# A two-layer trunk with eight experts on one core: earlier sums, transposed turns and four pieces ahead of the routing

## The chip, the cores and the metric

The kernel runs on one NeuronCore of a Trainium2 chip. The metric is the device time of one execution in microseconds (us), from the program's start to its end; lower is better. TensorE (PE in the profile; PEld is its weight load), VectorE (DVE), ScalarE (ACT), GpSimd (POOL) and SyncE (SP) run their own instruction lists and wait for each other by semaphores. SP issues the transfers of the weights.

## What is computed

Two layers over 256 latent and 256 context tokens of width 1024. Layer 0 ends in a dense feed-forward part, layer 1 in eight experts of which each latent token takes two. The change lies in the experts of layer 1 and in what stands right ahead of them:

```python
def swiglu(h, wg, wu, wd):
    return (jax.nn.silu(h @ wg) * (h @ wu)) @ wd

def moe_ffn(h, w_r, wg, wu, wd):
    logits = (h @ w_r).astype(jnp.float32)
    top_v, top_i = lax.top_k(logits, TOP_K)               # TOP_K = 2
    gates = jax.nn.softmax(top_v, axis=-1)
    combine = jnp.sum(jax.nn.one_hot(top_i, N_EXPERTS, dtype=jnp.float32) * gates[..., None], axis=-2).astype(h.dtype)
    out = jnp.zeros_like(h)
    for e in range(N_EXPERTS):                            # N_EXPERTS = 8
        out = out + combine[..., e:e + 1] * swiglu(h, wg[e], wu[e], wd[e])
    return out
...
x = x + mod[5] * f        # f = moe_ffn(hf, ...), hf of 256 x 1024; wg, wu 1024 x 2816, wd 2816 x 1024
```

## The kernel before

The first 878 us or so hold both layers up to the last output projection; then the routing ranks the experts by the number of their tokens, and from about 900 us on the experts run.

**Places.** The program is fixed while the routing is not, so experts are put on eight places with a capacity of slots each: place 0 has 160 slots (128, and 32 more that are called the rest, number NE), places 1 and 2 have 128, 3 to 5 have 64, 6 and 7 have 32. Place 7 is always expert 0, so its weights can be loaded before the routing is known. `gather` makes a place's tokens (`xe`) by one-hot products; AHEAD names the chunk at which each gather of a group of places begins.

**Chunks and pieces.** The 2816 hidden columns of an expert are 11 chunks of 256. A chunk takes three pieces of 1 MiB: two of gate and up (`gu`), one of down (`dn`); 264 pieces in all. SP issues them in the order of use (`Weights._load`, L240) into a ring of raw buffers: 4, and 5 more from one pool, hold pieces ahead of the routing, 3 more come with a pool that opens after it (`more`). For a wide place (128 slots) each piece is split in halves into a high part by ACT (`whi`, L275) and a low part by DVE (`wlo`, L276), in two pairs of buffers (tags `hi` and `lo`); a half is split when it is due. Narrow (32) and middle (64) places use the raw pieces.

**Rounds.** RUNS sets the order: `(None, (4, 0))` is four rounds with narrow chunks alone; `(1, (6, 11))` is run 1, the 11 chunks of place 1 with 6 narrow chunks (places 7, then 6) and 11 middle ones (3, 4, 5) spread over them; then run 0 and run 2, and two narrow rounds at the end. A round does the wide chunk's gate-up, the down product of the wide chunk of the round before, then narrow and middle gate-ups and the down products of the former round's, then the turns.

**Turns.** The gate-up of a narrow or middle chunk leaves its values folded over the partitions. They are copied to SBUF (`mid`), turned by TensorE into a bank `mTx` (`turn`: a product with the constant `sel` for 32 slots, which adds two folds on the way, and a transpose for 64), and made into `silx` by ACT's silu and DVE's product (`turned`, L1589). The wide chunk's `sil` is transposed into a bank `mT` and split into `mh` (ACT) and `ml` (DVE, L438).

**Finishes.** A place's down products add up over 11 chunks in a bank: `py` (two, one wide place at a time), `pys` (one, a middle place) or `pyx` (one, a narrow place). After the last, `finishes` is put among the side tasks, one finish at a time over all places (`finishing`). It multiplies the sum by mod5 (`y`, L1766 for wide, L1770 for others), splits it (`yh`, `yl`), and for each half and each 128 tokens scatters it by a one-hot product (`sc`, two banks by turns) that DVE adds to `acc` by the gate (L1780). A side task is moved on whenever the main order polls; where its instructions come in an engine's list is then fixed by the planner's clock (`o.clk`).

Of the kernel before, what the change touches and what calls it, by code (L numbers as in the profile page):

```python
# [18 lines left out]
P = 128  # L19
# [195 lines left out]
class Weights:  # L215


    def __init__(self, net, items, nraw, nhi):
# [3 lines left out]
        self.raw_live = self.hi_live = self.half = 0  # L222
        self.ring, self.at_ring = [(net.wp, nraw)] * nraw, 0
# [6 lines left out]
    def _load(self):  # L230
# [6 lines left out]
        pool, bufs = self.ring[self.at_ring]  # L237
        self.at_ring = (self.at_ring + 1) % len(self.ring)
        t = pool.tile([P, WW if pool is net.wp else 2048], F32, tag="raw", name="wraw", bufs=bufs)
# [7 lines left out]
    def more(self, pool, n):  # L247

        a = self.at_ring
        self.ring = self.ring[:a] + [(pool, n)] * n + self.ring[a:]  # L250
        self.nraw += n

# [88 lines left out]
class Net:  # L341
# [1150 lines left out]
    def onehot(self, p):  # L1492

        nc = self.nc
        yield from until(lambda: len(self.ohT) < 2)
# [10 lines left out]
        ohT = self.mp.tile([P, 2, P], F32R, tag="ohT", name="ohT", bufs=2)  # L1506
# [5 lines left out]
    YB, YH = 1, 1  # L1512
# [63 lines left out]
    def turn(self, pt, at, v, m):  # L1576
        for j in range(2):
            b = v[:, P * j:P * j + P]
            if m == 32:
                self.mm(pt[:, at + 64 * j:at + 64 * j + 64], b, self.sel, True, True)  # L1580
            else:
                self.tp(pt[:, at + P * j:at + P * j + P], b)

    def turned(self, pt, at, m):

        src = pt[:, at:at + 4 * m].rearrange("p (j g s) -> p j g s", j=2, g=2)
# [5 lines left out]
    def experts(self):  # L1592
# [6 lines left out]
        self.finishing = False  # L1599
        self.ndone = 0  # L1600
        self.sel = self.mp.tile([P, 64], F32, name="sel", bufs=1)
        nc.vector.tensor_tensor(self.sel, self.c("ident", 0, 64), self.c("swap", 0, 64), op=ALU.add)
        o.spawn(self.gather(0), 2)
        pw, pn = None, []
        for w, ns in self.rounds() + [(None, [])]:
# [71 lines left out]
            if mids:  # L1677
                pt, at = self.bank("mTx"), 0
                for *_, m, v in mids:
                    self.turn(pt, at, v, m)  # L1680
                    at += 4 * m
            pw = None
            if w:
                pm = self.bank("mT")
                for j in range(2):
                    self.tp(pm[:, P * j:P * j + P], sil[:, P * j:P * j + P])
                mh = self.mp.tile([P, 256], F32R, tag="mh", name="mh", bufs=1)
                ml = self.mp.tile([P, 256], F32R, tag="ml", name="ml", bufs=1)
                self.split(mh, ml, pm[:, :256])
                pw = [*w, mh, ml, None]  # L1690
            at = 0
            for p, c, m, v in mids:
                mx = self.turned(pt, at, m)
                at += 4 * m
                if p == NE:
                    pw[4] = mx
                else:
                    pn.append((p, c, mx))
            yield

    def down(self, p, c, mh, ml):
# [12 lines left out]
        if z and p:  # L1714
            self.o.spawn(self.finishes(p), 1)
        return w

    def down_rest(self, w, c, mx):
# [13 lines left out]
        if c == NCH - 1:  # L1732
            self.o.spawn(self.finishes(0), 1)

    def down_small(self, p, c, mx):
# [8 lines left out]
        if c == NCH - 1:  # L1744
            self.o.spawn(self.finishes(p), 1)

    def finishes(self, p):
        yield from until(lambda: not self.finishing)
        self.finishing = True
        for q in (p, NE) if p == 0 else (p,):  # L1750
            yield from self.finish(q)
        self.finishing = False

    def finish(self, p):

        nc = self.nc
        m = self.slots(p)
        parts = P // m
        w = 512 if m > 32 else 256
        yield from until(lambda: self.ohT.get(p) is not None)  # L1760
        ohT = self.ohT[p]
        for n in range(2 if m == P else 1):
            yh, yl = (self.mp.tile([P, 512], F32R, tag=nm, name=nm, bufs=self.YH) for nm in ("yh", "yl"))
# [8 lines left out]
            yield 3.0  # L1772
# [172 lines left out]
```

## Time and profile before

| | us |
|---|---|
| median of 3 runs | 1585.33 (1581.52 to 1587.26) |
| profiled execution | 1583.83 |
| its span, first to last instruction | 1582.1 |
| mean granted TensorE clock, as a share of full speed | 0.978 |
| TensorE, VectorE, ScalarE busy | 1500.2, 821.2, 666.7 |
| one MoE piece, issue to landing, median | 12.6 |

The rows are of one profiled execution. A busy row gives an instruction group's start and its length in us, engine, line, operation, output and inputs; the bracket at the end is the idle time before it on that engine and what ended it. TensorE's ends are modelled, so its pitch from start to start is safer than its lengths. [...]

### The profile page before, as it was taken

Reading aid. Unit: us, or ns where it says so; the run is one execution under the profiler, and the core shown is the slowest. Engines: PE = TensorE matmul, PEld = TensorE weight load, DVE = VectorE, ACT = ScalarE, POOL = GpSimd, SP = SyncE. Lnnn points to the kernel's source line nnn. Section 1 sums busy time; section 2 is a strip of 40 time slices with the busy share of each in tenths; the row PEclk is TensorE's granted clock in tenths of the full one; section 3 lists DMA queues with packets and bytes.
Section 4 is the critical chain, followed back from the end, with each engine's and each line's share of the span. In section 5 each row is a group of like instructions: output and inputs, shape, how many; then the busy total and the mean of one; then the engine's idle time right before and its main releaser. Section 6 shows DMA issues by size and latency. Waiting matters only on the chain. (4 is left out here: it accounts for less than half of the span.)

```text
span 1582.1 us, 23498 instructions
## 1 busy us (share of the span) xinstructions
PE 1500.2 (95%) x9302; PEld 1081.1 (68%) x9303; DVE 821.2 (52%) x1481; ACT 666.7 (42%) x1189; POOL 102.6 (6%) x135
## 2 busy tenths in 40 slices
PE   5999998899999999999999899999999999999997
PEld 1766675787887787878757776666566666656654
DVE  2687568543232333378774344544465444654545
ACT  3566644443222312266455354444343443433441
POOL 1200123210000000030300000000000000000000
PEclk9999999999999999999999899999999999999998
DMA  9422055333323323333164499999998999999994
GB/s 372 152 106 107 28 211 202 133 133 112 129 91 149 133 107 113 112 141 142 56 267 181 152 418 419 419 419 420 418 390 358 371 413 417 419 402 407 419 420 158
DMA packets 57715, 396.10 MB, mean 250 GB/s; under 512 B 6528, under 2 KB 8576, under 8 KB 10496
## 3 DMA queue, kind: packets, MB, share of 16 engines
q1 hardware_dynamic: 56016, 392.03, 62.2%
q10 hardware_dynamic: 1584, 2.52, 0.4%
q8 instruction: 75, 1.23, 0.3%
q14 instruction: 40, 0.33, 0.1%
HBM read 393.47 MB, written 1.05 MB: 249 GB/s over the span
## 5 line engine op out<-in xcount | busy, mean ns | idle before, releaser
L276 DVE TENSOR_TENSOR wlo<-wraw,whi 128x1024 fp32r<-128x1024 f32 (+2 forms) x318 | 377.0, 1222 | 161.2 <-ACT whi L275 155.9
L275 ACT ACTIVATE whi<-wraw 128x1024 fp32r<-128x1024 f32 (+2 forms) x318 | 320.0, 1047 | 148.5 <-PE fd L374 57.9
L374 PE MATMUL gu<-whi,xw 128*128 128x512 f32 x528 | 169.1, 401 | 4.2 <-ACT whi L275 4.2
L374 PE MATMUL gu<-wraw,xs 128*64 128x256 f32 (+1 forms) x1760 | 166.2, 386 | 0.5 <-ACT xs L1484 0.5
L374 PEld LDWEIGHTS gu<-wraw,xs 128*64 128x64 f32 (+1 forms) x1760 | 94.4, 127 | 64.3 <-issue 14.6
L374 PEld LDWEIGHTS gu<-whi,xw 128*128 128x128 f32 x528 | 96.9, 190 | 24.5 <-ACT whi L275 6.1
L374 PE MATMUL gu<-wlo,xw 128*128 128x512 f32 x264 | 104.9, 397 | 3.5 <-DVE wlo L276 3.5
L1162 DVE TENSOR_TENSOR fsil<-fsil,fu 128x512 f32<-128x512 f32 x22 | 15.1, 688 | 153.5 <-PE fu L374 118.2
L374 PE MATMUL pys<-wraw,silx 128*32 128x256 f32 (+1 forms) x616 | 87.6, 480 | 6.8 <-DVE y L1770 4.1
L425 ACT ACTIVATE fsil<-fg 128x512 f32<-128x512 f32 x22 | 13.1, 598 | 174.3 <-PE fg L374 174.3
L1573 ACT ACTIVATE mid<-gu 128x256 f32<-128x256 f32 x55 | 21.0, 382 | 137.1 <-PE gu L374 137.1
L374 PE MATMUL fg<-ahi,whi 128*128 128x512 f32 (+1 forms) x192 | 72.3, 377 | 0.0
L374 PE MATMUL fg<-alo,whi 128*128 128x512 f32 (+1 forms) x192 | 71.6, 373 | 0.2 <-POOL alo L523 0.2
L374 PE MATMUL fg<-ahi,wlo 128*128 128x512 f32 (+1 forms) x192 | 71.4, 372 | 0.0
L374 PE MATMUL fu<-alo,whi 128*128 128x512 f32 (+1 forms) x192 | 71.4, 372 | 0.0
L374 PE MATMUL fu<-ahi,wlo 128*128 128x512 f32 (+1 forms) x192 | 71.3, 372 | 0.0
L374 PE MATMUL fu<-ahi,whi 128*128 128x512 f32 (+1 forms) x192 | 71.3, 372 | 0.0
L374 PE MATMUL fd<-mhi,whi 128*128 128x512 f32 (+1 forms) x188 | 70.7, 376 | 0.0
L374 PE MATMUL fd<-mlo,whi 128*128 128x512 f32 (+1 forms) x188 | 70.6, 375 | 0.0
L374 PE MATMUL fd<-mhi,wlo 128*128 128x512 f32 (+1 forms) x188 | 70.6, 375 | 0.0
L374 PE MATMUL modp<-wraw,csil 128*32 128x512 f32 x384 | 56.7, 628 | 12.0 <-ACT csil L425 6.9
L374 PEld LDWEIGHTS gu<-wlo,xw 128*128 128x128 f32 x264 | 49.9, 189 | 18.3 <-DVE wlo L276 7.4
(342 smaller groups left out, 2831.8 us busy)
## 6 DMA issues: line engine op xcount, KB each, us to landing
wraw<-in_moe_dram SPq DMA_DIRECT2D x264, 1024.0 KB, 12.6
wraw<-in_wmod_dram SPq DMA_DIRECT2D x48, 1024.0 KB, 6.4
wraw<-in_fgu_dram SPq DMA_DIRECT2D x22, 1024.0 KB, 4.8
wraw<-in_win_dram SPq DMA_DIRECT2D x16, 1024.0 KB, 4.9
wraw<-in_wout_dram SPq DMA_DIRECT2D x8, 1024.0 KB, 6.2
wraw<-in_fdn_dram SPq DMA_DIRECT2D x8, 1024.0 KB, 6.2
wraw<-in_fdn_dram SPq DMA_DIRECT2D x4, 768.0 KB, 4.9
wraw<-in_wgd_dram SPq DMA_DIRECT2D x2, 1056.0 KB, 4.9
```

Of the source, the lines that this page charges most:

```text
L275: nc.scalar.activation(hi[:, cs], t[:, cs], AF.Copy)
L276: nc.vector.tensor_tensor(lo[:, cs], t[:, cs], hi[:, cs].bitcast(F32), op=ALU.subtract)
L374: self.nc.tensor.matmul(out, l, r, start=start, stop=stop)
L425: self.last_act = self.nc.scalar.activation(out, in_, func, **kw)
L1162: self.nc.vector.tensor_tensor(s, s, pu, op=ALU.mult)
L1573: self.nc.scalar.activation(v, ps[:, :256], AF.Copy)
```

## The change

1. RUNS puts six narrow rounds in front instead of four, and takes one out of run 1 and one out of run 2; place 7 then ends in the first round of run 0, where place 1 (by its chunk 10) and place 3 end as well. The gathers for places 1 and for 3 to 5 begin two chunks later.
2. Four more pieces of place 7 (numbers 9 to 12) are loaded ahead of the routing, into the buffers of the halves (`spare`), which phase A no longer uses by then.
3. A narrow chunk is turned by transposes of 128x128; ACT copies the two folds' first, DVE adds the second (`sum32`). Up to two turned things (a narrow or middle `mid`, and the wide `sil`) share one bank.
4. At a place's last down product its `y`, `yh` and `yl` are made at once (`halves`, `begin`), wide places' into a buffer of the tokens' pool (`fin`); a finish waits, inline, for the former finish of its kind (wide, or not) only. The last place's scatters wait for all others. There are three one-hot buffers (`ohT`), not two.
5. Four small constants of layer 0 (`csil`, `modT0`, `acoef`, `nsink`) move to a pool that is closed after phase A, which gives the room.

```diff
+        if self._room():
+            pool, bufs = self.ring[self.at_ring]
+            self.at_ring = (self.at_ring + 1) % len(self.ring)
+            t = pool.tile([P, WW if pool is net.wp else 2048], F32, tag="raw", name="wraw", bufs=bufs)
+        else:
+            t = self.spare.pop(0)()
+            self.spared.add(i)
...
-            while self.i_load < len(self.items) and self.i_load - min(self.raw, default=self.i_load) < self.nraw and \
+            while self.i_load < len(self.items) and (self._room() or self.spare) and \
...
-    AHEAD = {(7, 2): 1, (7, 3): 2, (1, 6): 3, (1, 8): 4, (0, 6): 5}
-    RUNS = ((None, (4, 0)), (1, (6, 11)), (0, (6, 11)), (2, (4, 11)), (None, (2, 0)))
+    AHEAD = {(7, 4): 1, (7, 5): 2, (1, 6): 3, (1, 8): 4, (0, 6): 5}
+    RUNS = ((None, (6, 0)), (1, (5, 11)), (0, (6, 11)), (2, (3, 11)), (None, (2, 0)))
...
-            if m == 32:
-                self.mm(pt[:, at + 64 * j:at + 64 * j + 64], b, self.sel, True, True)
-            else:
-                self.tp(pt[:, at + P * j:at + P * j + P], b)
+            self.tp(pt[:, at + P * j:at + P * j + P], v[:, P * j:P * j + P])
...
+        if m == 32:
+            v = src.rearrange("p (j r c) -> p j r c", j=2, r=2)
+            src = self.mp.tile([P, 2, 64], F32, tag="sum32", name="sum32", bufs=2)
+            self.nc.scalar.activation(src, v[:, :, 0, :], AF.Copy)
+            self.nc.vector.tensor_tensor(src, src, v[:, :, 1, :], op=ALU.add)
...
+            jobs = [[x, x[3]] for x in mids] + ([[None, sil]] if w else [])
+            for i, x in enumerate(jobs):
+                if i % 2 == 0:
+                    pt = self.bank("mT" if i + 1 == len(jobs) else "mTx")
+                self.turn(pt, 256 * (i % 2), x[1])
+                x[1] = pt
...
-            self.o.spawn(self.finishes(p), 1)
+            self.finished(p)
...
+    def finished(self, p):
+        self.o.wait(lambda: not self.finishing[self.wide(p)])
+        self.o.spawn(self.finishes(p), 1)
+        self.o.poll()
...
+        if p == self.last:
+            yield from until(lambda: self.ndone == NE)
...
+                self.w.spare = [lambda nm=nm: self.wp.tile([P, WW], F32, tag=nm, name="wraw", bufs=2) for nm in ("hi", "lo", "hi", "lo")]
+                self.w.advance()
                 self.route()
```

Three places in the engines' lists. First SP's list around the routing, where the registers that are loaded hold the routing's result; before:

```order
L240 DMA wraw<-in_wout_dram 128x2048 x4
L240 DMA wraw<-in_moe_dram 128x2048 x11
L1452 TENSOR_LOAD regs
L1452 ISA x2
L240 ISA
L240 DMA wraw<-in_moe_dram 128x2048
```

and in the changed kernel:

```order
L245 DMA wraw<-in_wout_dram 128x2048 x4
L245 DMA wraw<-in_moe_dram 128x2048 x17
L1461 TENSOR_LOAD regs
L1461 ISA x2
L245 ISA
L245 DMA wraw<-in_moe_dram 128x2048
```

Six more loads of place 7 stand ahead of the first register load: four in the halves' buffers, and two in the ring's.

Second TensorE's list in the first round of run 0, around place 3's last down product (`pys` of 64 rows; `sc` are scatters, `mTx` and `mT` the turns); before:

```order
L374 MATMUL gu<-wraw,xs_7655 64x256 x8
L374 MATMUL sc<-yh,ohT 128x512
L374 MATMUL sc<-yl,ohT 128x512
L374 MATMUL pys<-wraw,silx 64x512 x4
L374 MATMUL mTx<-sel,mid 128x64 x2
L379 MATMUL mTx<-const,mid 128x128 x2
L379 MATMUL mT<-const,sil 128x128 x2
L374 MATMUL gu<-whi,xw 128x512 x2
```

and in the changed kernel:

```order
L383 MATMUL pys<-wraw,silx 64x512 x4
L383 MATMUL sc<-fin,ohT 128x512 x2
L383 MATMUL sc<-yh,ohT 128x256
L383 MATMUL sc<-yl,ohT 128x256
L383 MATMUL sc<-fin,ohT 128x512 x2
L383 MATMUL sc<-yh,ohT 128x256
L383 MATMUL sc<-yl,ohT 128x256
...
L388 MATMUL mTx<-const,mid 128x128 x4
L388 MATMUL mT<-const,sil 128x128 x2
L383 MATMUL gu<-whi,xw 128x512 x2
```

The scatters of places 1 and 7 now stand between place 3's last down product and the round's turns (six more pairs of 256 follow the last one shown), and two transposes take the place of the products with `sel`.

Third DVE's list in the same round, whose `acc` additions free the scatters' banks; before:

```order
L1766 TENSOR_TENSOR y<-py,mod5row 128x512
L438 TENSOR_TENSOR yl<-y,yh 128x512
L1766 TENSOR_TENSOR y<-py,mod5row 128x512
L1780 SCALAR_TENSOR_TENSOR acc<-sc,gate,acc 128x512 x2
L276 TENSOR_TENSOR wlo<-wraw,whi 128x1024 x4
L438 TENSOR_TENSOR yl<-y,yh 128x512
L438 TENSOR_TENSOR ml<-mT,mh 128x256
```

and in the changed kernel:

```order
L1776 TENSOR_TENSOR y<-pys,mod5row 64x512
L1815 SCALAR_TENSOR_TENSOR acc<-sc,gate,acc 128x512
L1815 SCALAR_TENSOR_TENSOR acc<-sc,gate,acc 128x256
L1776 TENSOR_TENSOR y<-pys,mod5row 64x512
L285 TENSOR_TENSOR wlo<-wraw,whi 128x1024 x2
L1815 SCALAR_TENSOR_TENSOR acc<-sc,gate,acc 128x512
L285 TENSOR_TENSOR wlo<-wraw,whi 128x1024 x2
L1815 SCALAR_TENSOR_TENSOR acc<-sc,gate,acc 128x256 x6
L447 TENSOR_TENSOR yl<-y,yh 128x512
L447 TENSOR_TENSOR ml<-mT,mh 128x256
```

Place 3's `y` stands right behind its down product now, among the accumulations of places 1 and 7, and the four splits stand between them.

## Rows read from the trace of the kernel before

**Rows 1.** The page's first part: busy us, share of the span, instructions.
```profile
PE 1500.2 (95%) x9302; PEld 1081.1 (68%) x9303; DVE 821.2 (52%) x1481; ACT 666.7 (42%) x1189; POOL 102.6 (6%) x135
```
**Rows 2.** Stretches: length, busy PE, PEld, DVE, ACT, POOL, granted clock, DMA share, GB/s.
```profile
878.00:890.00 12.00, 9.58 (x73) 8.58 (x71) 2.15 (x5) 3.08 (x7) 0.00 (x0) 1.00 0.00 0
...
928.00:1118.00 190.00, 185.07 (x1245) 122.63 (x1243) 87.94 (x110) 83.74 (x137) 0.00 (x0) 1.00 1.01 419
1118.00:1134.00 16.00, 12.48 (x55) 8.15 (x58) 9.51 (x13) 7.46 (x12) 0.00 (x0) 0.89 1.01 419
1134.00:1212.00 78.00, 76.56 (x606) 47.33 (x596) 45.98 (x67) 30.64 (x50) 0.00 (x0) 1.00 0.93 379
...
1383.00:1391.00 8.00, 3.88 (x9) 1.04 (x10) 4.02 (x6) 1.33 (x2) 0.00 (x0) 0.65 1.01 419
```
**Rows 3.** TensorE's waits, 900 to 1582: us in total, times, longest.
```profile
PE gu L374 <- ACT whi L275: 4.2, 3, 2.4
PE pys L374 <- DVE y L1770: 4.1, 1, 4.1
...
PE sc L374 <- DVE ml L438: 0.7, 1, 0.7
```
**Rows 4.** Waits of the load queue, 1155 to 1290: us in total, times, longest.
```profile
SPq L240 <- PE gux L374: 79.1, 13, 14.7
```
**Rows 5.** TensorE at the start of run 0: start, length, group.
```profile
1120.42 0.73 PE L374 MATMUL gu<-whi,xw 128*128 128x512 f32 x2 [2.37 <-ACT whi L275]
...
1129.65 0.62 PE L374 MATMUL py<-whi,mh 128*128 128x512 f32 x2
1130.11 0.62 PE L374 MATMUL py<-whi,ml 128*128 128x512 f32 x2
```
**Rows 6.** ACT at the start of run 0.
```profile
1119.32 2.94 ACT L275 ACTIVATE whi<-wraw 128x1024 fp32r<-128x1024 f32 x3
```
**Rows 7.** TensorE in run 2: a middle place's down product and the turns of one round.
```profile
1459.52 1.89 PE L374 MATMUL pys<-wraw,silx 128*64 128x512 f32 x8
1461.34 0.66 PE L374 MATMUL mTx<-sel,mid 128*128 128x64 f32 x4
1461.84 0.39 PE L379 MATMUL mTx<-const,mid 128*128 128x128 f32 x2
1462.06 0.38 PE L379 MATMUL mT<-const,sil 128*128 128x128 f32 x2
```
**Rows 8.** Groups by form, 890 to 1582: busy us, mean ns of one, idle before.
```profile
L276 DVE TENSOR_TENSOR wlo<-wraw,whi 128x1024 fp32r<-128x1024 f32 x198 | 234.1, 1221 | 141.9 <-ACT whi L275 141.3
...
L374 PE MATMUL mTx<-sel,mid 128*128 128x64 f32 x132 | 20.2, 283 | 0.5 <-ACT mid L1573 0.5
L1780 DVE SCALAR_TENSOR_TENSOR acc<-sc,gate,acc 128x512 f32<-128x512 f32 x24 | 17.8, 750 | 28.0 <-PE sc L374 27.7
...
L1780 DVE SCALAR_TENSOR_TENSOR acc<-sc,gate,acc 128x256 f32<-128x256 f32 x24 | 11.4, 483 | 17.6 <-PE sc L374 17.6
...
L1589 DVE TENSOR_TENSOR silx<-silx,mTx 128x128 f32<-128x128 f32 x33 | 9.3, 282 | 6.9 <-ACT silx L425 6.9
L425 ACT ACTIVATE silx<-mTx 128x128 f32<-128x128 f32 x33 | 9.1, 275 | 11.8 <-DVE silx L1589 11.8
```
**Rows 9.** TensorE, ACT and DVE in the front rounds of place 7.
```profile
907.75 1.05 PE L374 MATMUL pys<-wraw,silx 128*32 128x256 f32 x16
...
909.42 0.22 ACT L425 ACTIVATE silx<-mTx 128x64 f32<-128x64 f32 x1 [1.04 <-PE mTx L374]
909.68 0.22 DVE L1589 TENSOR_TENSOR silx<-silx,mTx 128x64 f32<-128x64 f32 x1 [2.53 <-ACT silx L425]
...
911.06 1.05 PE L374 MATMUL pys<-wraw,silx 128*32 128x256 f32 x16
```
**Rows 10.** DVE, and TensorE, at the start of run 2.
```profile
1386.37 0.69 DVE L1770 TENSOR_TENSOR y<-pys,mod5row 64x512 f32<-64x512 f32 x1
...
1387.12 3.68 PE L374 MATMUL pys<-wraw,silx 128*64 128x512 f32 x8 [4.12 <-DVE y L1770]
```

More of the change, by code (lines that the diff above doesn't have):

```diff
@@ L251, in more, with _room @@
         self.nraw += n
+    def _room(self):
+        a = min(self.raw, default=self.i_load)
+        return self.i_load - a - sum(j >= a for j in self.spared) < self.nraw
     def _split(self, halves=2):
@@ L1494, in onehot @@
         nc = self.nc
-        yield from until(lambda: len(self.ohT) < 2)
+        yield from until(lambda: len(self.ohT) < 3)
         self.ohT[p] = None
@@ L1744, in down_small, with halves @@
         if c == NCH - 1:
[L1745 to L1757, printed above, removed]
+            self.finished(p)
+    def halves(self, p):
+        nc, m = self.nc, self.slots(p)
         parts = P // m
         w = 512 if m > 32 else 256
[L1760 to L1763, printed above, removed]
+        if m == P:
+            f = self.mp.tile([P, 2, KB, P], F32R, tag="xw", name="fin", bufs=2).rearrange("p a k s -> p (a k s)")
+            ys = [(f[:, 1024 * n:1024 * n + 512], f[:, 1024 * n + 512:1024 * n + 1024]) for n in range(2)]
+        else:
+            ys = [tuple(self.mp.tile([P, 512], F32R, tag=nm, name=nm, bufs=1) for nm in ("yh", "yl"))]
+        for n, (yh, yl) in enumerate(ys):
             y = self.mp.tile([P, 512], F32, tag="xsum", name="y", bufs=self.YB)
@@ new lines, in finishes, with begin, finish @@
+    def finishes(self, p):
+        yield from self.finish(p, self.begin(p))
+        if p == 0:
+            yield from until(lambda: not self.finishing[False])
+            yield from self.finish(NE, self.begin(NE))
+    def begin(self, p):
+        self.finishing[self.wide(p)] = True
+        return self.halves(p)
+    def finished(self, p):
+        self.o.wait(lambda: not self.finishing[self.wide(p)])
+        self.o.spawn(self.finishes(p), 1)
+        self.o.poll()
+    def finish(self, p, ys):
+        nc = self.nc
+        m = self.slots(p)
+        parts = P // m
+        w = 512 if m > 32 else 256
+        wide = m == P
+        yield max(3.0, self.w.splits - self.o.clk + 3.0)
+        yield from until(lambda: self.ohT.get(p) is not None)
+        ohT = self.ohT[p]
+        if p == self.last:
+            yield from until(lambda: self.ndone == NE)
+        for g in range(D // w):
+            cs = slice(w * g, w * g + w)
+            rows = slice(0, P) if wide else slice(m * g, m * g + m)
+            for t in range(2):
+                pz = self.bank("sc")
+                for i, v in enumerate(ys[g if wide else 0]):
+                    self.mm(pz[:, :w], ohT[rows, t, :], v[rows, :w], i == 0, i == 1)
+                nc.vector.scalar_tensor_tensor(self.acc[:, t, cs], pz[:, :w], self.gate[:, t, p:p + 1], self.acc[:, t, cs],
+                                               op0=ALU.mult, op1=ALU.add)
+                if p == self.last:
+                    nc.sync.dma_start(self.out[P * t:P * t + P, cs], self.acc[:, t, cs])
+                yield 1.0
```

83 lines of the change are left out of this document (33 added, 50 removed).

## The prediction

> **What bounds the kernel now.** I read the page's first part, then the busy times by stretch, then the engines' waits, and last the timelines where the waits are long. TensorE is busy 95% of the span [rows 1]. By stretch, the rounds of run 1 (928 to 1118) are nearly full, 185.07 us of 190.00, but the stretches at the start of run 0 (1118 to 1134) and of run 2 (1383 to 1391) are not: 12.48 of 16.00 and 3.88 of 8.00, at granted clocks of 0.89 and 0.65 of full [rows 2]. The list of TensorE's waits from 900 us on names ACT's halves (`whi`) and DVE's reading of a sum (`y`) first [rows 3]; none of its lines names a load. A second resource is almost as full: the DMA share is 1.00 or 1.01 in those three stretches, at 419 GB/s [rows 2], which is 2.50 us for a piece of 1 MiB (1,048,576 bytes over 419 GB/s). In run 0 it is 0.93 (1134 to 1212) [rows 2], and there the queue waits 79.1 us for TensorE's `gux` products to give buffers back [rows 4]. So in run 0 TensorE sets the pace and the stream follows; in the other runs the two are close. I take TensorE as the bound, and the stream as what is late next.
>
> **The change, part by part.**
>
> *Narrow chunks moved.* Six rounds of place 7 run in front before the first wide place, not four; one comes out of run 1, one out of run 2. A chunk's matmuls cost the same wherever they stand (3.31 us from one front `pys` to the next, 907.75 to 911.06 [rows 9]), so TensorE's sum is unchanged: 0. But a narrow chunk takes three pieces, 7.5 us of stream, in 3.31 us of work; two more of them in front want 15 us of stream sooner. What covers that is the next part.
>
> *Four pieces ahead of the routing.* From 878 to 890 us the DMA moves nothing (share 0.00) [rows 2], because all 9 raw buffers hold pieces and the next three come with the pool that opens after routing. Four pieces at 2.50 us are 10.0 us and fit in those 12.00, if the halves' buffers are free by then. With them, 10.0 us of stream and 6.6 us of longer work stand against the 15 us: covered. I take 0 for the front; the bounds are −10 (the pieces without effect) and +2.
>
> *Plain turns.* A turn of a narrow chunk was two products with `sel` in 0.50 us from its start to the next (1461.34 to 1461.84), where the two transposes that follow take 0.22 (1461.84 to 1462.06) [rows 7]. There are 132 records at four to a turn, so 33 turns [rows 8]. Eight of them (six in front, two at the end) wait for their `mid` anyhow; 25 × 0.28 = 7.0 us. What is added: a copy of 128x128 on ACT and an addition of 128x128 on DVE, which the trace has as like forms at 275 and 282 ns [rows 8], with two hand-overs; one such, from ACT's 909.42 + 0.22 to DVE's 909.68, took 0.04 [rows 9], and I allow up to 0.2: 0.6 to 0.95 us behind each turn. In front the product ends at 909.68 + 0.22 = 909.90 and the down product that reads it starts at 911.06 [rows 9], so 1.16 us of slack hide it. In the runs a wide gate-up of 24 matmuls at 0.23 us lies between (two in 0.46, 1129.65 to 1130.11 [rows 5]), 5.6 us. Cost 0 under that cover; 0.95 for each round without it.
>
> *Start of run 0.* ACT begins the splits of place 0's first piece only at 1119.32 [rows 6], behind the middle values of the round before; TensorE waits 2.37 us for the first half, and then takes from 1120.42 to 1129.65, 9.2 us, for a piece pair of 5.6 [rows 5]. Lost: 2.37 + 3.6 = 6.0, of which some is the low clock. In the order no split of that piece stood ahead of `mh`; now two do. The first two halves are then there and the other two run beside their use; a stall of up to 1 us may be left. I take +5.
>
> *Start of run 2.* Place 5's first down product waits 4.12 us, until 1387.12, for the bank of place 4's sum, which DVE reads in two pieces behind place 0's finish, the last at 1386.37 + 0.69 [rows 10]; the down product then takes 3.68 us where 1.89 is usual [rows 7, 10], at a clock of 0.65 [rows 2]. Now a place's `y` is read at its last down product. 4.12 + 1.79 = 5.9, and about 0.6 for the slow turn behind it: +6.5. If the bank stays in use, 0.
>
> *Finish in run 0.* One scatter's wait of 0.7 for `ml` [rows 3], which comes from the split in the middle of a finish, goes: +0.7.
>
> *The block at round (0,0).* Places 7, 1 and 3 now end in one round, so their scatters stand in a row. Behind place 3's last down product DVE has, by its order, two `y` at 0.69 [rows 10], two `acc` of 512 at 0.750, seven of 256 at 0.483 and four splits at 1.221 [rows 8]: 1.4 + 1.5 + 3.4 + 4.9 = 11.2 us. TensorE has two pairs of 512, seven of 256 and six transposes: 4 × 0.23 + 14 × 0.12 + 6 × 0.11 = 3.3 us by the bare matmuls, and I take 5 with the change of weights. With two banks the last scatter waits for the accumulation two before it, and the transposes come behind: about 11.6 us, so 6.5 of waiting. A wait of 4.12 us was followed by a down product at half speed [rows 10]; I add 2 for that: −8.5. Bounds: 0 (the splits run beside earlier work) and −11.
>
> [...] At the start of run 2 the clock was at 0.65 over the stretch with the wait [rows 2]. [...]
>
> *Tail.* Places 2's and 5's scatters come mostly before place 6's last down product now, four accumulations at 0.750 [rows 8] or 3.0 us; place 6's own turn is longer by up to 0.95 and its scatters wait for all others. +1, from −1 to +3.
>
> **Sum.** 7 + 5 + 6.5 + 0.7 − 8.5 + 1 = 11.7 us less, against the profiled execution of 1583.83. The median of the runs is 1585.33, 1.5 above it; I take the gain off the median: 1573.6. The bounds of block, front, starts and tail will not all be met on one side; together they give roughly 1564 to 1586. A measurement of this kernel can tell 0.5%, 7.9 us, from no change.
>
> **Rivals.**
>
> *The stream is the bound.* For it: shares of 1.00 over 190 us [rows 2]. Then what TensorE saves is spent waiting for loads, and only the earlier pieces count: 4 × 2.50 = 10.0 us, so 1575.3. Against it: no wait of TensorE names a load, and the queue waited for buffers [rows 4]. [...]
>
> *The block eats the gain.* At its bound of −11, and with the halves that are now made at once ahead of other work on DVE (4 × 0.69 = 2.8 exposed): 11.7 − 2.5 − 2.8 = 6.4, so 1578.9. For it: DVE works its list in order, and a finish now puts `y` ahead of splits. Against: that much of the block's list are splits that TensorE needs anyhow.
>
> *The early pieces come too late.* If the halves' buffers come free only near 890, the front starves: −10, 1.7 left, 1583.6. Against it: in the 12 us before 890 DVE has 2.15 us of work [rows 2], so the last split had long been made.
>
> *Slower: the added link is exposed.* ACT's copy and DVE's addition stand ahead of their next splits. If the splits behind them are what TensorE waits for, 0.95 × 33 = 31.4 us are lost against 11.7, so 1605. It outweighs the gain from 13 exposed links on (13 × 0.95 = 12.4), and costs over 0.5% from 21 on. For it: the wait of 2.37 us came from just that order of `mh` and splits [rows 5, 6]. Against: in most rounds of the runs the order shows two to four halves of the next piece ahead of `mh`.
>
> **How the numbers follow.** Forecast 0.50, with its own range of 1564 to 1581; stream 0.18; block 0.15; late pieces 0.08; slower 0.09. Faster by over 0.5% (under 1577.4): four fifths of the forecast and of the stream, and some of the block, 0.62; slower (over 1593.3), 0.09; within, 0.29. The range of 1564 to 1586 takes in all but the slower rival and the best ends of the bounds.
>
> **What would show it.** Right: no wait over 1 us at the starts of run 0 and run 2, with the clock near 1.00; turns at 0.22; four more loads landed by 892; a block of about 11 us at round (0,0) with waits for `acc`. Wrong: waits of TensorE that name `wraw` (the stream or late pieces), waits for `silx` or for `whi` in many rounds (the link), or the old stalls at another place.

## The result, and the profile after

The changed kernel takes 1591.6 us (median of 7 runs, 1590.88 to 1594.22); the kernel before, run beside it, 1583.54. The ratio is 1.0052, with a 95% interval of 1.0037 to 1.0068: slower by about 8 us, where 1573.6 was forecast, outside the range of 1564 to 1586. The first part of the page of the changed kernel stands against [rows 1]:

```profile
span 1589.9 us, 23449 instructions
...
PE 1501.9 (94%) x9236; PEld 1076.2 (68%) x9237; DVE 829.5 (52%) x1513; ACT 675.8 (43%) x1222; POOL 102.4 (6%) x135
```

TensorE's busy time did not fall, although it issues 66 instructions less. Where the time went is seen by stretches. The table is worked out from the starts of single matmuls in the two traces: the routing's `pos` product, the first gate-up matmuls of places 1, 0 and 2, that of place 2's last chunk (round (2,10)), and the last end on TensorE. So "run 2" is its first ten rounds, and "end" is the last one and what follows. The forecast's terms are put to the stretch in which they should have shown, with 3.3 us for each narrow chunk moved and 0.28 for each turn (5 in run 1, 17 in run 0, 3 in run 2).

| stretch (us) | before | after | change | forecast | missed by |
|---|---|---|---|---|---|
| front (`pos` to place 1's gate-up) | 36.20 | 45.57 | +9.37 | +6.6 | +2.8 |
| run 1 | 191.87 | 195.04 | +3.17 | −3.3 − 1.4 | +7.9 |
| run 0 | 230.62 | 230.83 | +0.21 | −5 − 0.7 + 8.5 − 4.8 | +2.2 |
| run 2 | 178.08 | 167.84 | −10.24 | −3.3 − 6.5 − 0.8 | +0.4 |
| end | 47.32 | 47.85 | +0.53 | −1 | +1.5 |
| sum | 684.09 | 687.12 | +3.03 | −11.7 | +14.7 |

Two pairs of traces give the noise of such a stretch, since their kernels issue the same instructions with buffers at other addresses: the kernel before and e1 (below) differ by up to 1.6 us in one stretch, the changed kernel and e2 by 0.1. So the misses of the front and of run 1 are the clear ones; those of run 0, run 2 and the end are not far from noise. What comes ahead of the routing's product took 892.35 before and 897.18 after, 4.83 more, for which the forecast had no term. So run 2 came as forecast, run 1 did not, and something happened in the part that the change only seemed to prepare.

The stretches of the changed kernel, with the columns of [rows 2]; 881 to 897 is ahead of the routing, 942 to 1137 is run 1 and 1036 to 1103 its rounds (1,6) to (1,8), 1158 to 1178 is the block at round (0,0), 1386 to 1394 the start of run 2:

```profile
881.00:897.00 16.00, 11.83 (x90) 10.74 (x88) 4.61 (x20) 5.42 (x11) 0.00 (x0) 0.95 0.71 274
...
942.00:1137.00 195.00, 184.70 (x1172) 121.07 (x1172) 94.11 (x118) 88.29 (x141) 0.00 (x0) 0.97 0.99 404
1036.00:1103.00 67.00, 61.12 (x401) 41.79 (x398) 28.93 (x38) 30.30 (x54) 0.00 (x0) 0.95 1.00 412
...
1158.00:1164.00 6.00, 3.03 (x12) 1.18 (x8) 5.08 (x7) 1.44 (x2) 0.00 (x0) 1.00 1.01 423
1164.00:1171.00 7.00, 3.96 (x15) 3.17 (x16) 6.03 (x10) 0.63 (x1) 0.00 (x0) 0.57 0.70 289
1171.00:1178.00 7.00, 7.00 (x23) 5.14 (x22) 2.39 (x7) 2.98 (x6) 0.00 (x0) 0.70 0.00 0
...
1386.00:1394.00 8.00, 6.52 (x28) 4.59 (x27) 7.89 (x13) 2.95 (x5) 0.00 (x0) 1.00 1.01 418
```

In run 1 the clock is at 0.97, and at 0.95 in those three rounds, where the kernel before had 1.00 [rows 2], and TensorE stands idle for 10.3 of 195 us, 5.9 of them in the three rounds, where it was 4.9 of 190. The start of run 2 has its clock at 1.00. TensorE's waits from 900 us on, against [rows 3]:

```profile
PE gu L383 <- ACT whi L284: 8.7, 4, 3.0
PE sc L383 <- DVE acc L1815: 6.3, 7, 3.1
PE gu L383 <- DVE wlo L285: 5.3, 11, 1.2
PE pys L383 <- DVE silx L1602: 4.7, 3, 2.8
```

The wait for `y` is gone. The gate-up's wait for the halves has doubled, 4.2 to 8.7 us, and moved: none of it is left at the start of run 0; 2.5 us of it stand in front, 5.1 in run 1 and 1.2 in run 2. ACT, then TensorE, at the first gate-up of place 1 and at round (1,6):

```profile
940.06 0.91 ACT L1493 ACTIVATE xs<-xe,modT,sc 128x192 f32<-128x192 f32 x2 [0.39 <-PE xe L383]
...
941.65 3.88 ACT L284 ACTIVATE whi<-wraw 128x1024 fp32r<-128x1024 f32 x4
...
942.75 0.93 PE L383 MATMUL gu<-whi,xw 128*128 128x512 f32 x2 [2.51 <-ACT whi L284]
```

```profile
1042.52 1.50 ACT L1493 ACTIVATE h<-xe,modT,sc 128x128 f32<-128x128 f32 x4 [2.42 <-PE xe L383]
...
1045.51 1.50 ACT L1493 ACTIVATE h<-xe,modT,sc 128x128 f32<-128x128 f32 x4 [0.82 <-DVE xw L447]
1047.05 0.63 ACT L446 ACTIVATE xw<-h 128x512 fp32r<-128x512 f32 x1
1047.58 1.99 ACT L284 ACTIVATE whi<-wraw 128x1024 fp32r<-128x1024 f32 x2
...
1048.68 1.04 PE L383 MATMUL gu<-whi,xw 128*128 128x512 f32 x2 [3.01 <-ACT whi L284]
```

In both places ACT works for a gather (`xs`, `h`, `xw`), with idle time of its own between the steps, and only then makes the halves. That is no matter of loads: the piece needed at 1048.68 had landed at 1029.5. ACT made the halves where they stand in its list, from 1047.58 on, behind the gather's steps, though it had been idle for 2.42 and 0.82 us ahead of those.

### The profile page after: what moved, and what is told of

It is laid out like the page before. It is cut to its first block, busy times and chain, and to the rows that moved or that the text cites. A ratio compares the mean times of both kernels' runs of the same rounds, so it can differ in the third digit from the quotient of the medians.

```text
span 1589.9 us, 23449 instructions
## 1 busy us (share of the span) xinstructions
PE 1501.9 (94%) x9236; PEld 1076.2 (68%) x9237; DVE 829.5 (52%) x1513; ACT 675.8 (43%) x1222; POOL 102.4 (6%) x135
## 5 line engine op out<-in xcount | busy, mean ns | idle before, releaser
L383 PE MATMUL gu<-whi,xw 128*128 128x512 f32 x528 | 172.3, 408 | 8.7 <-ACT whi L284 8.7
```

The costliest lines, as they stand in the source:

```text
L383: self.nc.tensor.matmul(out, l, r, start=start, stop=stop)
```

## The experiments

The theory at this point: (A) the halves are put too late in ACT's list, and each part of the change moves something in front of them. The rivals: (B) the move of the constants is itself what costs, since the part ahead of the routing is longer; (C) the two gathers of run 1 now fall into rounds that have a narrow chunk, (1,6) and (1,8), which had none before; (D) the finishes' new order costs more than it gives. Each median stands beside that of the kernel before, run on the same chip at the same time.

### The parts alone

**e1_alloc**: the kernel before with the constants moved, nothing else.

```diff
-            self.nsink = keep.tile([P, 16], F32, name="nsink")
...
+                self.nsink = self.ka.tile([P, 16], F32, name="nsink")
```

(and the same for `csil`, `modT0`, `acoef`)

> The kernel before, with only the four constants of layer 0 moved to the pool that closes after phase A. Theory 1 (addresses): this moves the weights' buffers down by 1728 bytes per partition while the moving operand ahi of the feed-forward stays where it is, and that slows fg and fu: their mean length goes from 390 to about 395 ns as in the changed kernel, fd stays at 389, phase A ends about 5 us later, and the time is about 5 us (0.3%) above before. Rival (the chip or the run was slower when the changed kernel was profiled): fg and fu stay at 390 ns, phase A ends as before, ratio 1.000.

1587.35 against 1583.54, ratio 1.003 (1.0014 to 1.0045). The move alone costs about 4 us, with the same instructions. A single execution does not show it well, since the part ahead of the routing varies by itself: `pos` starts between 888.9 and 892.8 us in the seven traces with the constants in their old place, between 893.5 and 897.2 in the three with the move and no padding (e1, e3 and the changed kernel), and between 890.1 and 895.4 in the nine with the padding of the next run.

**e2_pad**: the changed kernel, 320 bytes of padding in that pool.

```diff
-                self.nsink = self.ka.tile([P, 16], F32, name="nsink")
+                self.nsink = self.ka.tile([P, 96], F32, name="nsink")[:, :16]
```

> The changed kernel, with 320 bytes of padding per partition behind the moved constants, so that the distance between ahi and the weights' buffers differs from that of before by 2048 bytes and not by 1728. Theory 1 (addresses, by their place within some power of two up to 2048): fg and fu return to 390 ns, phase A ends about 5 us earlier than in the changed kernel, time about 1586.5. Rival (only the very distance counts, or addresses do not matter): fg and fu stay at 394 to 396 ns, time 1591.6.

1586.97, ratio 1.003 (1.0011 to 1.0049), 4.6 under the changed kernel; the two intervals overlap, so the size is uncertain. Its time from the routing's product on is that of the changed kernel (687.15 and 687.12), so the gain lies ahead of it. A group of the dense feed-forward part of layer 0 (300 to 680 us, by form: busy us, mean ns) tells what it is, in the kernels before, after, e1 and e2, in this order:

```profile
L374 PE MATMUL fg<-ahi,wlo 128*128 128x512 f32 x160 | 62.3, 390 | 0.0
```

```profile
L383 PE MATMUL fg<-ahi,wlo 128*128 128x512 f32 x160 | 63.3, 396 | 0.0
...
L383 PE MATMUL fd<-mhi,whi 128*128 128x512 f32 x163 | 63.5, 389 | 0.0
```

```profile
L374 PE MATMUL fg<-ahi,wlo 128*128 128x512 f32 x160 | 63.4, 396 | 0.0
```

```profile
L383 PE MATMUL fg<-ahi,wlo 128*128 128x512 f32 x160 | 62.3, 390 | 0.0
```

With the constants moved, a gate or up matmul takes 4 to 7 ns longer (six such groups, 0.6 to 1.1 us each); with the padding it is back. The down matmuls (`fd`) stay at 389. The four constants hold 1728 bytes of a partition. By the addresses in the built programs, the weights' buffers moved down by as much while `ahi`, the moving operand, stayed; `fd`'s operand moved along with the weights. So (B) holds, as one part. The six groups make some 5 us of busy time. What property of the distance matters was not tried.

**e6_turns**: the kernel before with the plain turns alone.

```diff
-            if m == 32:
-                self.mm(pt[:, at + 64 * j:at + 64 * j + 64], b, self.sel, True, True)
-            else:
-                self.tp(pt[:, at + P * j:at + P * j + P], b)
+            self.tp(pt[:, at + P * j:at + P * j + P], v[:, P * j:P * j + P])
...
+            self.nc.scalar.activation(src, v[:, :, 0, :], AF.Copy)
+            self.nc.vector.tensor_tensor(src, src, v[:, :, 1, :], op=ALU.add)
```

> The kernel before with the new turns alone (transposes, ACT's copy, DVE's addition, shared bank); runs, finishes and allocation are those of before. The forecast's term: 7 us less, 1576.5, from rounds with a rest or narrow chunk that are each 0.25 us shorter or more, with no new waits. Rival (the added copy and addition are exposed, 0.95 us in many rounds): 1584 or more, with waits for whi or silx in more rounds than before.

1584.76 against 1583.35, ratio 1.0004 (0.9992 to 1.0016): the 7 us of shorter turns don't show. By its trace they are there in the second part of run 0 (139.13 to 136.65 over seven rounds) and are lost elsewhere: front +2.6, run 1 +1.0, run 2 +3.8. In front the down product waits 2.83 us for `silx`, not 2.00. In run 2, round (2,6), ACT, TensorE and three stretches (columns as above):

```profile
1461.67 0.27 ACT L1586 ACTIVATE sum<-mTx 128x128 f32<-128x128 f32 x1
...
1462.78 2.94 ACT L275 ACTIVATE whi<-wraw 128x1024 fp32r<-128x1024 f32 x3
...
1463.88 0.73 PE L374 MATMUL gu<-whi,xw 128*128 128x512 f32 x2 [1.17 <-ACT whi L275]
1465.14 0.52 PE L374 MATMUL gu<-wlo,xw 128*128 128x512 f32 x1 [0.53 <-DVE wlo L276]
...
1463.00:1465.00 2.00, 0.73 (x2) 0.30 (x2) 1.35 (x3) 2.00 (x3) 0.00 (x0) 1.00 1.01 406
1465.00:1467.00 2.00, 1.86 (x5) 1.53 (x6) 2.00 (x3) 1.18 (x2) 0.00 (x0) 0.62 1.00 414
1467.00:1469.00 2.00, 2.00 (x6) 1.52 (x6) 1.58 (x2) 0.60 (x1) 0.00 (x0) 0.52 1.03 426
```

and the same round of the kernel before:

```profile
1464.76 0.73 PE L374 MATMUL gu<-whi,xw 128*128 128x512 f32 x2 [0.91 <-ACT whi L275]
...
1466.00:1468.00 2.00, 1.98 (x9) 1.63 (x10) 2.00 (x2) 1.58 (x2) 0.00 (x0) 1.00 1.00 414
```

The folds' copy (`sum`) and the silu behind it stand ahead of the halves. The wait is 0.26 us longer, but the clock falls to 0.62 and 0.52 behind it, and the round takes 19.69 us, not 17.84. Round (2,9) of e6 and round (2,8) of the changed kernel have the same two waits and take 19.69 us as well.

**e3_turnfin**: the changed kernel without the moved chunks and the early pieces.

```diff
-    AHEAD = {(7, 4): 1, (7, 5): 2, (1, 6): 3, (1, 8): 4, (0, 6): 5}
-    RUNS = ((None, (6, 0)), (1, (5, 11)), (0, (6, 11)), (2, (3, 11)), (None, (2, 0)))
+    AHEAD = {(7, 2): 1, (7, 3): 2, (1, 6): 3, (1, 8): 4, (0, 6): 5}
+    RUNS = ((None, (4, 0)), (1, (6, 11)), (0, (6, 11)), (2, (4, 11)), (None, (2, 0)))
```

> The changed kernel with RUNS and AHEAD of before and without the four early pieces: turns, finishes and allocation are those of the change. Theory 2 (the loss lies in the front and in run 1, where the early pieces hold the halves' buffers and gathers stand ahead of splits): run 1 is as short as before or shorter (about 190 us), the wait of 2.5 us at the first wide round is gone, and the time is about 1578: +5 for phase A, -11 for turns, starts and finishes. Rival (the added copy and addition in each turn cost the time): the time stays at 1590 or above and run 1 at 195 us.

1591.67, ratio 1.0069 (1.0046 to 1.0092), as slow as the whole change. The wait for `y` at the start of run 2 is gone in it, and is still 4.12 us in e6 and in e4 below, so the finishes removed it. The start of run 0 still has its wait (2.58 us). And a wait of another sort stands in round (0,0), after which three gate-up matmuls take 1.28 us from start to start (1158.59 to 1159.87), where 0.69 is usual (1467.06 to 1467.75 in the kernel before); TensorE, and what DVE did then:

```profile
1151.83 4.63 DVE L285 TENSOR_TENSOR wlo<-wraw,whi 128x1024 fp32r<-128x1024 f32 x4
...
1157.57 1.22 PE L383 MATMUL sc<-fin,ohT 128*128 128x512 f32 x2 [5.51 <-DVE ml L447]
1158.59 1.05 PE L383 MATMUL gu<-whi,xw 128*128 128x512 f32 x2
```

The scatter wants a bank that the turn still holds until DVE has made `ml`, and `ml` stands behind four splits.

**e4_runs**: the kernel before with the moved chunks and the early pieces alone.

```diff
-    AHEAD = {(7, 2): 1, (7, 3): 2, (1, 6): 3, (1, 8): 4, (0, 6): 5}
+    AHEAD = {(7, 4): 1, (7, 5): 2, (1, 6): 3, (1, 8): 4, (0, 6): 5}
...
-    RUNS = ((None, (4, 0)), (1, (6, 11)), (0, (6, 11)), (2, (4, 11)), (None, (2, 0)))
+    RUNS = ((None, (6, 0)), (1, (5, 11)), (0, (6, 11)), (2, (3, 11)), (None, (2, 0)))
...
+                self.w.spare = [lambda nm=nm: self.wp.tile([P, WW], F32, tag=nm, name="wraw", bufs=2) for nm in ("hi", "lo", "hi", "lo")]
+                self.w.advance()
```

> The kernel before with the new RUNS and AHEAD and the four early pieces; turns, finishes and allocation are those of before. Theory 2: fg and fu at 390 ns, but waits for whi of 2 to 3 us at the first wide round and in the rounds of run 1 with gathers, the first wide round 9 us later than before and run 1 no shorter although it has a narrow chunk less: about 1590. Rival (moving the chunks costs nothing, the turns do): within 2 us of before, 1584.

1597.41, ratio 1.0094 (1.0064 to 1.0125). Front +8.5, and runs 1 and 2, each a chunk of 3.3 us shorter in work, take 3.3 and 0.8 us more. The start of run 0 has no wait in it, so there it is the new order of the rounds that helps. Alone the moved chunks cost 14 us; on top of turns, finishes and move of the constants (after against e3) nothing. So the parts cannot be added up, and (D) falls as the sole cause: this kernel has the old finishes and is slower still. Which of the other parts keeps the moved chunks from costing more was not tried apart.

### Gathers and early pieces

**e5_gathers**: e2 with four of the five gathers begun one round earlier, those of run 1 so in rounds without a narrow chunk.

```diff
-    AHEAD = {(7, 4): 1, (7, 5): 2, (1, 6): 3, (1, 8): 4, (0, 6): 5}
+    AHEAD = {(7, 3): 1, (7, 4): 2, (1, 5): 3, (1, 7): 4, (0, 6): 5}
```

> The changed kernel with the padding of the run before it, and with four of the five gathers one chunk earlier: (7,3), (7,4), (1,5) and (1,7) in place of (7,4), (7,5), (1,6) and (1,8), so that in run 1 they fall into rounds without a narrow chunk, as they did before. Theory 2 (in the changed kernel ACT's work for a gather stands ahead of halves that TensorE needs at once): the waits for whi of 3.0 and 2.6 us in run 1 fall to those of before (1.7 and 0.8), the one of 2.5 at the first wide round goes, run 1 is some 4 us shorter and the time about 1581, 6 below the padded kernel. Rival (the narrow chunk in the round is not what matters, the waits move along): run 1 stays at 195 us, time 1587.

1587.12, ratio 1.0024 (1.0008 to 1.004), the same as e2. The loss moves with the gathers: rounds (1,5) and (1,7) take 20.99 and 29.46 us, where in e2 rounds (1,6) and (1,8) took 25.45 and 24.55. (C) falls.

**e7_nospare**: e2 without the early pieces.

```diff
-                self.w.spare = [lambda nm=nm: self.wp.tile([P, WW], F32, tag=nm, name="wraw", bufs=2) for nm in ("hi", "lo", "hi", "lo")]
-                self.w.advance()
```

> The changed kernel with the padding, without the four early pieces. The forecast's reading (the early pieces feed the front): the front and run 1 starve, waits of TensorE name loads, time 1592 to 1597. Theory 2 (the early pieces hold the buffers that the first wide round's halves need): the wait of 2.5 us at the first wide round goes, and what the stream loses is hidden in part, time 1585 to 1589.

1585.99, ratio 1.0014 (1.0002 to 1.0026): the early pieces are worth nothing here that can be told from noise. They do arrive: the DMA share from 881 to 897 is 0.71 in the changed kernel, and the four land from 886.37 to 896.32, 8 to 12 us before theirs in the kernel before. The load was not what the front waited for. Without the early pieces the halves' buffers are free, and the wait at the first gate-up of place 1 falls from 2.51 to 0.51 us. But the halves stand behind the gather there too (from 936.56), a wait of 2.74 for a `mid` behind the other gather comes in, and the front takes 46.68 us, 1.1 more than in e2. Over the whole of front and run 1 the pieces are worth 3.4 us, and run 0 takes 3.2 of that back.

### Splitting earlier

If (A) is right, the planner's rule for when a half is due is the place to turn. First the plainest form.

**e9_early, e10_after_early, e11_turns_early, e12_turnfin_early**: a half is due as soon as its buffers are free; in the kernel before, in e7, in e6, and in e3 with the padding.

```diff
-        return net.o.clk > self.land[i] and net.o.clk > self.splits - net.SPLIT / 2
+        return True
```

> The kernel before with one line of the planner changed: a half is split as soon as one of its two pairs of buffers is free, not when the planner's clock says that it is due; by the order all four halves of a wide round's gate-up then stand ahead of the values (mh) of the round before. Theory 3 (the waits for whi and wlo come from where the halves stand in ACT's and DVE's lists, not from the transfers): the stall of 5.8 us at the start of run 0 and most waits for whi and wlo (4.2 + 3.5 us) go, about 1575. Rival (halves were late because pieces were, or early halves push back what TensorE needs more): ACT waits for loads, or waits for silx, acc and y grow; 1583 or more.

> The changed kernel, padded, without the early pieces, with the same line changed. Theory 3: the waits of run 1 (12 us idle without early pieces) fall to a few, the block at round (0,0) shrinks as its four splits are made before it; 1586 less about 10, 1576. Rival: the block stays, as accumulations now stand behind splits elsewhere; 1584.

> The kernel before with the new turns and the same line changed. Theory 3 (the added copy costs only where it stands ahead of halves that TensorE waits for): with all halves ahead of it the turns give what the forecast counted, 7 us less than the kernel before with that line alone, about 1568. Rival (the turns gain nothing anyhow): the same time as that kernel.

> Turns, finishes and allocation of the change, padded, with the old runs and no early pieces, and the same line changed. The forecast's terms for the finishes (start of run 2 +6.5): 5 us below the kernel with turns and early halves, about 1563. Rival (a finish made at once puts y and its halves in DVE's list ahead of splits, and the scatters then wait for banks): at or above that kernel.

1626.21, 1612.69, 1628.76 and 1606.71 against 1583.82: ratios 1.0281, 1.0192, 1.0294 and 1.014. All much slower. ACT's and TensorE's waits in e9, from 920 us on:

```profile
ACT whi L275 <- DMA wraw<-in_moe_dram: 30.2, 16, 7.4
```

```profile
PE gu L374 <- DVE sil L1632: 35.9, 12, 4.8
```

ACT now waits for pieces that haven't landed, and the silu that TensorE needs stands behind. The theory in the form "the earlier the better" fell. What remained was that a gate-up half, which the next round begins with, is put late, and a down half need not be early.

**e13_gu, e14_turns_gu, e15_turnfin_gu**: only gate-up halves are due early, from 5 us before the planner has them landed and without regard to how many splits are ahead; in the kernel before, in e6, and in e3 with the padding.

```diff
-        return net.o.clk > self.land[i] and net.o.clk > self.splits - net.SPLIT / 2
+        return net.o.clk > self.land[i] - (5.0 if self.items[i][0][0] == "gu" else 0.0) and (self.items[i][0][0] == "gu" or net.o.clk > self.splits - net.SPLIT / 2)
```

> The kernel before, with the planner's rule changed for gate-up pieces only: their halves are split from 5 us ahead of the planner's landing time on, down pieces as before. By the order all four gate-up halves of a round stand ahead of mh, and ahead of the product sil no more than the two down halves that are needed next. Theory 3b (what costs is that gate-up halves stand behind turns and gathers; splitting everything early failed because halves then stood ahead of sil and because ACT waited for loads): the waits for whi and wlo of 4.2 + 3.5 us and the stall at the start of run 0 go, about 1576. Rival (there is no slack on ACT and DVE for it, or the pieces have not landed): ACT waits for loads and the time is 1584 or more.

> The same rule, with the new turns. Theory 3b: the added copy no longer stands ahead of halves that TensorE waits for, so the turns give 5 to 7 us on top of the kernel with the rule alone, about 1570. Rival (the added copy and addition cost as much as the transposes save, wherever the halves stand): no difference to the kernel with the rule alone.

> The same rule with turns, finishes and padded allocation of the change, old runs and no early pieces. Forecast's terms for the finishes: the start of run 2 gives 6 us, the block at the start of run 0 with its own wait of 5.5 us for a bank takes them back unless its splits are made earlier: between 1566 and 1572, at least not above the kernel with turns and the rule. Rival (DVE's list with y ahead of splits makes the scatters wait for banks as before): 5 us above that kernel.

1581.61, 1578.21 and 1572.75 against 1583.62: ratios 0.9994 (0.9982 to 1.0007), 0.9971 (0.9954 to 0.9988) and 0.9937 (0.9916 to 0.9958). The rule alone changes nothing that can be measured, against the 8 us expected: run 1 is 2.7 us shorter in e13, but run 0 is 6.6 longer. With the rule the turns are worth 3.4 us (e13 to e14) and the finishes 5.5 (e14 to e15), by the medians; each pair's intervals overlap a little. The waits of the gate-up for `whi`, 4.2 us before, are gone in all three.

**e16_turnfin_r12, e18_nospare_r12, e17_all_r12**: the same rule, but in run 0 for its first chunk only (there the pieces come later); in e3 with the padding, in e7, and in e2, which is the whole change.

```diff
-        return net.o.clk > self.land[i] and net.o.clk > self.splits - net.SPLIT / 2
+        gu = self.items[i][0][0] == "gu" and (self.items[i][0][1] != 0 or self.items[i][0][2] == 0)
+        return net.o.clk > self.land[i] - (5.0 if gu else 0.0) and (gu or net.o.clk > self.splits - net.SPLIT / 2)
```

> The fastest kernel so far (turns, finishes, padded allocation, old runs, no early pieces, gate-up halves early), with the rule not applied to place 0 after its first chunk, where by the order of before four halves stood ahead of mh already. Theory 3b: rounds (0,4) to (0,10) return from 138.9 to 136.5 us, and the time is about 2 us lower, 1570.5. Rival (that stretch is set by the loads): no change, 1572.7.

> The same without the four early pieces. If the pieces feed the front, it is slower than with them, up to 10 us, and waits name loads; if they only hold the halves' buffers, it is 1 to 3 us faster, as the pair without the rule was (1585.99 against 1586.97).

> The whole change (new runs, early pieces, turns, finishes), padded, with the same rule. Tells what the moved chunks and the early pieces are worth once the halves are in place. Theory 3b (the loss of the moved chunks was the late halves in run 1): as fast as the kernel with the old runs or faster by the 2.6 us of the stall at the start of run 0, 1568 to 1572. Rival (the moved chunks themselves cost, by the early pieces in the halves' buffers and by run 1 having less work to cover gathers): 4 us or more above it, 1575 or more.

1570.44, 1569.36 and 1563.92 against 1583.06: ratios 0.9914 (0.9886 to 0.9942), 0.9923 (0.9894 to 0.9951) and 0.9865 (0.983 to 0.99). So with the halves in time the moved chunks alone give about 1 us, which cannot be told from noise, but the early pieces 5.4 (e18 to e17; their intervals overlap a little, and e17 has four runs, 1556.81 to 1568.2). By the traces they do so in run 1, 187.96 and 179.86 us. The last is the fastest kernel of the study and beats both. Its page, a stretch of run 1 and its waits from 890 us on:

```profile
span 1566.4 us, 23451 instructions
...
PE 1485.2 (95%) x9236; PEld 1079.9 (69%) x9237; DVE 828.2 (53%) x1513; ACT 676.7 (43%) x1222; POOL 103.2 (7%) x135
```

```profile
938.00:1118.00 180.00, 175.40 (x1180) 120.83 (x1180) 88.70 (x117) 87.53 (x142) 0.00 (x0) 1.00 1.01 419
...
PE mTx L389 <- ACT mid L1583: 5.7, 5, 1.9
PE pys L384 <- DVE silx L1603: 4.7, 3, 2.8
PE sc L384 <- DVE acc L1816: 3.7, 6, 1.9
PE py L384 <- ACT whi L284: 3.2, 3, 2.6
```

No gate-up waits for `whi`, the clock of run 1 is at 1.00, and run 1 takes 179.86 us, where the changed kernel took 195.04. TensorE's busy time is 16.7 us below the changed kernel's for the same number of matmuls; some 5 of these are the padding's (the six groups above), and 9.3 lie in run 1 (175.40 here, 184.70 there, with the clock at 1.00 and 0.97). The DMA share is 1.01 over those 180 us, as it was in run 1 of the kernel before; that the early pieces shorten run 1 speaks for the stream as what comes next there.

What this edit of the rule takes off, in one of its two forms and by the medians against the kernel before run beside them, is 2 us in the kernel before (e13), 7 in the one with the turns (e6 to e14), 16 in the whole change without the early pieces (e7 to e18), 23 in the whole change (e2 to e17). The more of the change is in, the more the order of the halves is worth.

## Why the prediction was wrong, step by step

**The bound: right in the main.** TensorE's time and its waits set the end; no wait of it in the changed kernel names a load, and the early pieces, worth 10 us by the stream's rival, gave nothing (e7). With the halves in time they give 5.4 us (e18 to e17), as "what is late next" had it.

**Narrow chunks, "0", and the front, "covered": wrong.** The cover was sought in the stream, 10.0 and 6.6 us against 15. But the front waits for halves, not for loads: 2.51 us at 942.75, with the `silx` wait grown from 2.00 to 2.83. The first wide chunk's two gate-up pieces had landed by 920.97, and the early pieces in the halves' buffers were used up by 922.3, but ACT makes the halves only from 941.65 on, behind both gathers, although it stands idle for 4.01 us ahead of 935.88: it is the order in the list, by the planner's rule, that is late. The early pieces in the halves' buffers are not the cause of it: without them the front is no shorter (e7). The term was not just too small; the wrong resource was asked. The front lost 2.8 us; with the halves put first (e17) it takes 42.93 us, 6.7 more than before, as the 6.6 had it.

Run 1, where ACT's gather work stands the same way, has two such waits, 3.01 us at 1048.68 and 2.06 at 1088.27, with a clock of 0.50 behind them (1050 to 1052 and 1091 to 1093). Against e17, whose run 1 has the same work, it takes 15.2 us more: 8.3 in those two rounds, 2.0 in the first, and 5.1 in rounds (1,2) to (1,5), where the clock is at 1.00 and no wait is longer than 0.53. So the order of the halves costs a little in every round, too, and there the kernel before paid as well.

**Plain turns, +7 with "Cost 0 under that cover": the saving right, the cover wrong.** Over seven rounds of run 0 with 11 such turns they gave 2.5 us (e6), 0.23 each where 0.28 was forecast. The addition behind a turn was costed for the one who reads it, with 5.6 us of gate-up between. It was not costed for what stands behind it on ACT: the halves of that same gate-up. e6 shows it at 1463.88, and e13 to e14 that with the halves put ahead about 3.4 of the 7 come out. The rival "the added link is exposed" had this mechanism, and with it the right side of zero. It got 0.09, on the ground that two to four halves stood ahead of `mh` in most rounds. Its price was wrong as well: not 0.95 in each of 33 rounds but some 7 us in all, paid in front, in a few rounds of run 2, where a wait of 1.17 us was followed by a clock of 0.62 and 0.52, and little by little in run 1, whose rounds (1,2) to (1,5) take 68.3 us in e6, 67.2 in the kernel before and 62.6 in e14.

**Start of run 0, +5: right.** TensorE goes from `mT` at 1137.65 straight to the gate-up at 1137.79; one wait of 1.24 for `wlo` is left at 1142.70. From the wait's start to the first `py` it took 11.6 us before and takes 7.3, so 4.3 us came. **Start of run 2, +6.5, and the finish, +0.7: right.** Run 2 is 10.24 us shorter, where 10.6 were forecast; one wait of 1.44 is left, at a clock of 1.00. e3, e4 and e6 show that the finishes removed the wait for `y`. With the old rounds they give only about half of the term: in e3 gate-ups wait 1.11 and 0.87 us for halves right there, and the first four rounds of run 2 take 76.6 us, 79.9 before (78.0 in e1) and 72.6 in the changed kernel.

**The block, −8.5: right.** From the scatters' start to the next gate-up it is 12.46 us, where 11.6 were forecast, with the two waits that the two banks make:

```profile
1158.71 0.73 PE L383 MATMUL sc<-fin,ohT 128*128 128x512 f32 x2
...
1164.57 0.38 PE L383 MATMUL sc<-yh,ohT 32*128 32x256 f32 x1 [3.13 <-DVE acc L1815]
...
1167.24 0.58 PE L383 MATMUL sc<-yh,ohT 32*128 32x256 f32 x1 [2.16 <-DVE acc L1815]
...
1171.17 1.20 PE L383 MATMUL gu<-whi,xw 128*128 128x512 f32 x2
```

Both waits lie behind pairs of splits on DVE (1161.38 and 1164.43, 2.36 and 2.35 us). The clock falls to 0.57 and is at 0.70 up to 1178, a little more than the 2 us allowed.

**Tail, +1: not seen.** The end took 0.53 us more, which is within the noise of a stretch.

**Moved constants: no term at all.** Part 5 of the change stood in the text of the change and got no sentence in the sum, as if a buffer's address had no price. e1 puts it at about 4 us (2 to 7 by its interval), half of the loss.

**The sum.** By the medians, 4 us of the 8 are the addresses (e1). The other 4 are what is left of the turns, finishes, moved chunks and early pieces. Once the halves stand in time, turns, finishes and early pieces gain 3.4, 5.5 and 5.4 us and the moved chunks hardly anything (e13 to e18); when they don't, all lose or stand still (e3, e4, e6, e7). That the order of the halves is the common cause is shown by the one edit that takes 16 us from e7 and 23 from e2; how the rest splits between the parts depends on which is taken first, and stays open.

## What to carry to other kernels

Before a step is called hidden, look not only at who reads its result but at what stands behind it on its own engine: in e6 the halves behind ACT's copy came later, and round (2,6) took 19.69 us, not 17.84. Where a change saves work on the busiest engine and the kernel's time does not fall, look for the short list of places at which a supply (here the halves) is put behind new work, and move the supply first; the same change went from 0.5% slower to 1.35% faster by that alone and the padding. And give every part of a change a term, the memory layout too, or build it alone.

## What the runs showed of the hardware

*Addresses and the pace of matmuls.* With the weights' buffers moved by 1728 bytes in a partition against the moving operand, the gate and up matmuls of 128x512 in layer 0 took 394 to 403 ns where they had taken 389 to 396 (the changed kernel and e1 against the kernel before; from start to start, in the means of the groups, 232 to 235 in the changed kernel and 227 to 228 before), at a clock of 1.00 in these two and with 0.0 us of idle time ahead of these groups; with 320 bytes of padding it was 389 to 396 again (e2).

*A little more waiting and the clock.* Behind waits of 0.91 and 0.53 us, one after the other, the granted clock stayed at 1.00 in round (2,6) of the kernel before; 1.17 and 0.53 at the same place in e6 were followed by stretches at 0.62 and 0.52. The longer wait cost 0.26 us by itself, and the round 1.85.
